# A hybrid decoder layer with the left pools of SBUF moved by 128 bytes, other homes for the split weights of the output projection, and an FFN issued stream by stream

## The chip, the cores and the metric

One core of a Trainium2 chip. The metric is the device time of one execution in microseconds; the time given for a kernel is the median of its runs.

## The reference

One layer over 1024 tokens of width 1024, in float32:

```python
h = rmsnorm(x, norm1_w) * (1 + scale1) + shift1          # scales, shifts, gates: silu(c) @ w_ada + b_ada
qa, ka, va, iq, ik, iw, qr, kr, vr, gr, ga, gb = split(h @ w_in)
y_a = sparse_attention(qa, ka, va, top 256 keys by iq, ik, iw) @ w_attn_proj
y_r = (silu(gr) * groupnorm(retention(qr, kr, vr))) @ w_ret_proj
x = x + gate1 * ((sigmoid(ga) * y_a + sigmoid(gb) * y_r) @ w_out)
h2 = rmsnorm(x, norm2_w) * (1 + scale2) + shift2
x = x + gate2 * ((silu(h2 @ w_ffn_gate) * (h2 @ w_ffn_up)) @ w_ffn_down)   # d_ff = 2816
return rmsnorm(x, final_norm_w)
```

## The kernel before

**Split operands.** Every large product is made of three matmuls on fp32r tiles: a float32 operand is split into a rounded part (`hi`, written by ACT) and the rest (`lo`, written by POOL or DVE), and hi·hi, hi·lo and lo·hi are summed in PSUM. Names that end in `hi` and `lo` are such parts. Nearly all of them are 128 x 128 stationary by 128 x 512 moving, called 512-column matmuls here.

**Who sets the order.** The kernel is written for a tile framework. A scheduler reorders the instructions of every engine, so the code's order is not the program's; each engine then runs its own list in order, and SP's list issues nearly all DMAs.

**Where tiles lie.** Pools grow from two ends of each partition's memory, "left" and "right". In the built program before, the tiles of the left pools that concern us (`whi`, `wlo`, `mhi`, `aT_hi`, `khi`, `fhi`, `flo`, `dw`, `wraw`) start at multiples of 256 bytes; the right pools' (`hT`, all slabs: `hc`, `early`, `late`, `raws`, `draw`, `dslot`) start 128 bytes after one. `qst`, in a left pool that is opened after some smaller tiles, also starts 128 bytes after one.

**Stages**, by the profile's time: condition vector and indexer projection to 123 us; indexer scores, projections from `w_in` (`hT` times `whi`, `wlo`) and retention with DVE's top-k to about 650; gates, retention projection and its normalisation (`gT`) to 907; attention to 1034; its projection to 1078; output projection (`w_out`) and second norm from 1083 to 1190; gate and up projections of the FFN from there to 1691; down projection to 1902.

**Output projection** (`for hf in range(2)`): `w_out` is loaded in 128 x 512 pieces to `wraw`, multiplied on POOL by the gate and split. The pieces of `hf` 0 use the ring of `whi`/`wlo` slots (`RING = 9`), which the attention's projection used before; of `hf` 1, four go to a slab tile `late`. `split_merged` makes `mhi` (ACT) and `mlo` (DVE), the other operand. In `hf` 1 each of the eight token tiles is normalised, transposed on PE and written by ACT to `hraw`.

**FFN, gate and up.** A Strassen-like scheme: `d_ff` is cut into 11 pairs, each with two streams (gate and up) of seven products (`ORDER` M1, M5, M6, M3, M7, M2, M4) of 12 matmuls. A product needs a combination of activations (`COMBOS`, tiles `hc`: h11, h21, S1, S2, h22, S4, S3) and a factor, 128 x 512 of weights or of differences of weights (`tmp`, by DVE, from `raws`), split to `fhi` (ACT) and `flo` (POOL), of which there are four slots each. M1 and M2 of pairs 0 and 1 are computed ahead: pair 0's factors (`early`) lie in slab 0 and are split while the output projection runs; pair 1's are split at the FFN's start into `fhi`/`flo` slots. The combinations S1 to S4 need the last token tile; DVE computes the sums (`hs`), ACT and POOL or DVE split them.

**What ends a pair.** `gu_finish` applies silu (ACT), multiplies gate by up (DVE), forms the four sums of activations for the down projection's own scheme and stores seven tiles to DRAM (`act_d`). `down_weights` loads a pair of rows of `w_ffn_down` to the one `dw` buffer (two loads of 512 KB), combines them in four DVE subtractions (L1167 to L1170) and stores 1 MB (`dw_d`). In the program the scheduler has put all eleven of these between about 1325 and 1460 us.

**Down projection.** `draw` loads, splits to `dslot` (ACT L1240; POOL or DVE L1241), products M1, M5, M6, M3, M7, M4, then M2, then the final norm (`sqh` squares, `rs3`).

Of the kernel before, what the change touches and what calls it, by code (L numbers as in the profile page):

```python
# [16 lines left out]
P = 128  # L17
# [24 lines left out]
def tile_hybrid_layer(ctx: ExitStack, tc: tile.TileContext, x, c, w_ada, b_ada, norm1_w, w_in,  # L42
# [20 lines left out]
    def f32(ap):  # L63
        return ap.bitcast(F32)
# [3 lines left out]
    def split_weight(raw, n, order=None):  # L68
        hi = ring.tile([P, H], R, name="whi", tag="whi", bufs=RING)
        lo = ring.tile([P, H], R, name="wlo", tag="wlo", bufs=RING)  # L70
# [8 lines left out]

    def raw_tile():  # L80
        return ring.tile([P, H], F32, name="wraw", tag="wraw", bufs=3)
# [779 lines left out]
    RING = 9  # L861
# [45 lines left out]
    COMBOS = {"h11": 3, "h21": 4, "S1": 1, "S2": 6, "h22": 0, "S4": 5, "S3": 2}  # L907
# [16 lines left out]
    hraw = [slab_tile(i, [P, 2, 4, H], F32, f"hraw{i}") for i in (2, 5)]  # L924
# [50 lines left out]
    def slab_slots():  # L975
        t = slab_tile(0, [P, 4, 2, H], R, "early")
        return lambda i: (four(t[:, i, 0, :]), four(t[:, i, 1, :]))

    for hf in range(2):
        cs = slice(hf * H, (hf + 1) * H)  # L980
        slots = []
        late = slab_tile(6, [P, 4, 2, H], R, "late") if hf else None
        for k in range(KT):
            if hf and k < 4:
                raw = raw_tile()
                nc.sync.dma_start(out=raw, in_=w_out[k * P:(k + 1) * P, cs])
                nc.gpsimd.tensor_mul(raw, raw, gate[:, cs])
                nc.scalar.activation(late[:, k, 0], raw, AF.Copy)
                nc.gpsimd.tensor_sub(late[:, k, 1], raw, f32(late[:, k, 0]))
                slots.append((late[:, k, 0], late[:, k, 1]))  # L990
            else:
                slots.append(rows_slot([(w_out, hf * H, H)], k, H, gate[:, cs]))
# [4 lines left out]
        for t in range(NT):  # L997
# [17 lines left out]
            for g in range(2):  # L1015
                xn = ring.tile([P, H], F32, name="xn2", tag="wraw", bufs=3)
# [11 lines left out]
            if t == 4:  # L1028
                early_load(0)
                early_split(0, slab_slots())  # L1030
            if t == 5:
                early_load(1)
    st_f.close()
# [95 lines left out]


# [58 lines left out]
    for p in range(2):  # L1189
        if p:  # L1190
            early_split(p, lambda i: factor_slot())
# [197 lines left out]
```

## Time and profile before

| | us |
|---|---|
| median of 3 runs | 1902.97 (1902.75 to 1904.68) |
| profiled execution | 1911.45 |
| its span | 1909.7 |
| PE busy in the span | 1781.0 (93%) |
| POOL, DVE, ACT busy | 898.0, 1183.3, 699.6 |

The profiled execution is one run with the hardware profiler on. Its span runs from the first to the last recorded instruction, and 1.75 us of its time lie outside. PE's mean granted clock is 0.975 of full speed. "Idle before" in square brackets is the time an engine did nothing ahead of a row, with what ended it.

### The profile page before, as it was taken

What the parts mean: (1) busy time and instruction counts of PE and PEld (TensorE: products, weight loads), DVE (VectorE), ACT (ScalarE), POOL (GpSimd) and SP (SyncE); (2) the same over time, 40 slices, a digit from 0 to 9 for tenths busy, and PEclk for the clock granted to TensorE, in tenths of its full rate; (3) what the DMA queues carried; (4) which work ended last, traced back from release to release, by engine and by line L of the source; (5) the groups of instructions that cost most, each with busy time, mean ns of one, the idle gap of its engine ahead of it and who ended that gap; (6) DMA issues with size and microseconds to landing.
All of it is one profiled execution on the core that took longest, in us unless ns stands there. A gap on an engine that the chain in (4) does not pass through costs nothing. (4 is left out here: it accounts for less than half of the span.)

```text
span 1909.7 us, 24906 instructions
## 1 busy us (share of the span) xinstructions
PE 1781.0 (93%) x8534; PEld 1445.4 (76%) x8534; DVE 1183.3 (62%) x1989; ACT 699.6 (37%) x1413; POOL 898.0 (47%) x954
## 2 busy tenths in 40 slices
PE   5899999999999998979899999599889999999997
PEld 4798888888888776867678787477667777788886
DVE  7646459999989784142665645856555444375554
ACT  3435432333322121210674246433233333354434
POOL 4572114665844372210463614844334444475585
PEclk9999999999999998989999999799999999999999
DMA  9443222122122775684944500235665333187652
GB/s 290 145 106 102 67 85 59 45 69 59 39 57 83 185 228 164 183 224 139 240 103 154 199 1 23 66 111 204 226 220 176 95 104 94 66 282 220 183 176 99
DMA packets 192286, 256.53 MB, mean 134 GB/s; under 512 B 29528, under 2 KB 126240, under 8 KB 189728
## 3 DMA queue, kind: packets, MB, share of 16 engines
q1 hardware_dynamic: 192160, 254.94, 43.8%
q8 instruction: 67, 1.10, 0.2%
q14 instruction: 59, 0.48, 0.1%
HBM read 190.67 MB, written 64.23 MB: 133 GB/s over the span
## 5 line engine op out<-in xcount | busy, mean ns | idle before, releaser
L73 POOL TENSOR_TENSOR wlo<-wraw,whi 128x512 fp32r<-128x512 f32 (+3 forms) x164 | 200.4, 1231 | 342.8 <-ACT whi L72 322.7
L108 PE MATMUL mm<-whi,hT_hi 128*128 128x512 f32 (+2 forms) x624 | 235.4, 379 | 7.1 <-ACT whi L72 6.0
L109 PE MATMUL mm<-wlo,hT_hi 128*128 128x512 f32 (+2 forms) x624 | 231.0, 370 | 0.8 <-POOL wlo L73 0.8
L110 PE MATMUL mm<-whi,hT_lo 128*128 128x512 f32 (+2 forms) x624 | 231.3, 371 | 0.0
L953 POOL TENSOR_TENSOR flo<-tmp,fhi 128x512 fp32r<-128x512 f32 x88 | 118.8, 1351 | 158.2 <-ACT fhi L952 126.2
L419 DVE MAX8 m<-score 128x8 f32<-128x384 f32 (+5 forms) x192 | 170.6, 891 | 4.7
L1111 PE MATMUL ya<-hc,fhi 128*128 128x512 f32 x344 | 140.1, 407 | 31.0 <-ACT fhi L952 20.6
L422 DVE MATCH_REPLACE8 score<-m,score 128x384 f32<-128x384 f32 (+5 forms) x192 | 168.1, 876 | 0.0
L72 ACT ACTIVATE whi<-wraw 128x512 fp32r<-128x512 f32 (+3 forms) x164 | 95.7, 593 | 192.4 <-DMA wraw<-in_w_in_dram 75.6
L1241 POOL TENSOR_TENSOR dslot<-draw,dslot 128x512 fp32r<-128x512 f32 x77 | 112.8, 1473 | 64.0 <-ACT dslot L1240 63.8
L108 PEld LDWEIGHTS mm<-whi,hT_hi 128*128 128x128 f32 x624 | 118.7, 190 | 27.2 <-ACT whi L72 6.6
L1113 PE MATMUL ya<-hc,fhi 128*128 128x512 f32 x344 | 139.0, 404 | 0.0
L1115 PE MATMUL ya<-hc,flo 128*128 128x512 f32 x344 | 136.3, 401 | 0.3 <-POOL flo L953 0.3
L115 PE MATMUL mm<-hT_hi,whi 128*128 128x512 f32 x328 | 123.8, 409 | 13.0 <-DVE qk_split L620 7.3
L953 POOL TENSOR_TENSOR flo<-raws,fhi 128x512 fp32r<-128x512 f32 x62 | 87.2, 1409 | 102.0 <-ACT fhi L952 102.0
L109 PEld LDWEIGHTS mm<-wlo,hT_hi 128*128 128x128 f32 x624 | 118.8, 190 | 20.6 <-POOL wlo L73 1.6
L110 PEld LDWEIGHTS mm<-whi,hT_lo 128*128 128x128 f32 x624 | 118.6, 190 | 19.6
L1241 DVE TENSOR_TENSOR dslot<-draw,dslot 128x512 fp32r<-128x512 f32 x77 | 79.5, 1047 | 84.4 <-ACT dslot L1240 74.4
L1240 ACT ACTIVATE dslot<-draw 128x512 fp32r<-128x512 f32 x154 | 89.4, 625 | 107.3 <-PE ya L1257 42.7
L117 PE MATMUL mm<-hT_lo,whi 128*128 128x512 f32 x328 | 124.8, 404 | 1.2 <-POOL hT_lo L247 1.2
L119 PE MATMUL mm<-hT_hi,wlo 128*128 128x512 f32 x328 | 123.5, 402 | 0.0
L952 ACT ACTIVATE fhi<-tmp 128x512 fp32r<-128x512 f32 x88 | 55.6, 631 | 177.9 <-PE yb L1113 69.6
(321 smaller groups left out, 4339.8 us busy)
## 6 DMA issues: line engine op xcount, KB each, us to landing
draw<-act_d SPq DMA_DIRECT2D x77, 256.0 KB
mw<-in_w_ada_dram SPq DMA_DIRECT2D x32, 512.0 KB
act_d<-c SPq DMA_DIRECT2D x62, 256.0 KB
wraw<-in_w_in_dram SPq DMA_DIRECT2D x56, 256.0 KB
wraw<-in_w_in_dram SPq DMA_DIRECT2D x96, 128.0 KB
raws<-in_w_ffn_gate_dram SPq DMA_DIRECT2D x24, 512.0 KB
raws<-in_w_ffn_up_dram SPq DMA_DIRECT2D x24, 512.0 KB
dw<-in_w_ffn_down_dram SPq DMA_DIRECT2D x22, 512.0 KB
```

Source lines behind the costliest of these rows:

```text
L73: nc.gpsimd.tensor_sub(lo[:, :n], raw[:, :n], f32(hi[:, :n]))
L108: nc.tensor.matmul(ps, lhsT=ahi, rhs=whi[:, :n], start=(i == 0), stop=False)
L109: nc.tensor.matmul(ps, lhsT=ahi, rhs=wlo[:, :n], start=False, stop=False)
L110: nc.tensor.matmul(ps, lhsT=alo, rhs=whi[:, :n], start=False, stop=(i == last))
L117: nc.tensor.matmul(ps, lhsT=whi, rhs=alo, start=False, stop=False)
L419: ins = nc.vector.max(m8, sc)
L422: nc.vector.match_replace(out=sc, in_to_replace=m8, in_values=sc, imm_value=TAKEN)
L953: nc.gpsimd.tensor_sub(lo, src, f32(hi))
L1111: nc.tensor.matmul(ps, lhsT=whi[:, k, :], rhs=hhi[:, k, :], start=first, stop=False, skip_group_check=True)
L1113: nc.tensor.matmul(ps, lhsT=whi[:, k, :], rhs=hlo[:, k, :], start=False, stop=False, skip_group_check=True)
L1115: nc.tensor.matmul(ps, lhsT=wlo[:, k, :], rhs=hhi[:, k, :], start=False, stop=last, skip_group_check=True)
L1241: lo_eng.tensor_sub(slot[:, 1], raw, f32(slot[:, 0]))
```

## The change

**Addresses.** `rs3`, a 64-byte tile in the first left pool, has four buffers for two. All left pools behind it start 128 bytes later: in the built program, the tiles of the left pools listed above start 128 bytes after a multiple of 256, as the right ones do (which have not moved). `qst` now starts at a multiple of 256, `khi` 128 after one.

**Output projection.** The pieces of `hf` 0 are split into slabs 2 and 5 (`wslot`), those of `hf` 1 into the ring, now of 8; `wraw` has four buffers for three. `hraw` takes slabs 2 and 5 only after that. Pair 1's early factors are split into slab 6 at token tile 5, and the slabs of S2, h22, S4 and S3 change places.

**FFN.** S4 has tiles of its own. Each stream's loads are issued one stream ahead. What ended a pair is spread: `after` applies silu or the multiplication behind the product that completes a block, and `finish_tasks` and `down_weights` queue the rest in `todo`, of which two are issued behind each later product.

**End.** `sqh` takes its buffers from the twelve `quad` tiles; second halves and norms of M4's tiles are issued after all four sums.

```diff
-    def split_weight(raw, n, order=None):
-        hi = ring.tile([P, H], R, name="whi", tag="whi", bufs=RING)
-        lo = ring.tile([P, H], R, name="wlo", tag="wlo", bufs=RING)
+    def split_weight(raw, n, order=None, home=None):
+        if home is not None:
+            hi, lo = home[:, 0], home[:, 1]
+        else:
...
-    RING = 9
+    RING = 8
+    N_RAW = 4
...
-    COMBOS = {"h11": 3, "h21": 4, "S1": 1, "S2": 6, "h22": 0, "S4": 5, "S3": 2}
+    COMBOS = {"h11": 3, "h21": 4, "S1": 1, "S2": 0, "h22": 6, "S4": 2, "S3": 5}
...
-    def slab_slots():
-        t = slab_tile(0, [P, 4, 2, H], R, "early")
+    def slab_slots(p):
+        t = slab_tile((0, 6)[p], [P, 4, 2, H], R, "early")
...
-        late = slab_tile(6, [P, 4, 2, H], R, "late") if hf else None
+        homes = [slab_tile(i, [P, 4, 2, H], R, "wslot") for i in (2, 5)] if hf == 0 else None
         for k in range(KT):
...
+            raw = raw_tile()
+            nc.sync.dma_start(out=raw, in_=w_out[k * P:(k + 1) * P, cs])
+            nc.gpsimd.tensor_mul(raw, raw, gate[:, cs])
+            home = homes and homes[k // 4][:, k % 4]
+            slots.append(split_weight(raw, H, home=home))
...
             if t == 5:
                 early_load(1)
+                early_split(1, slab_slots(1))
...
+        def after(self, m):
+            done = {"M3": "12", "M7": "22", "M2": "11", "M4": "21"}.get(m)
+            for c in [done] if done else []:
+                if c == "11" and self.p < 2:
+                    continue
+                self.use(c)
+            if m == "M4":
+                if self.p < 2:
+                    self.use("11")
+                if self.u:
+                    finish_tasks(self.p)
+        def use(self, c):
+            if self.u == 0:
+                src = self.A if c == "21" else self.c[c]
+                if c == "21":
+                    self.c[c] = quad_tile("c21")
+                nc.scalar.activation(self.c[c], src, AF.Silu)
+            else:
+                a = streams[self.p, 0].c[c]
+                nc.vector.tensor_mul(a, a, self.A if c == "21" else self.c[c])
...
-    def gu_finish(p, g, u):
-        a = {}
-        for b in ("12", "22", "11"):
-            nc.scalar.activation(g.c[b], g.c[b], AF.Silu)
-            nc.vector.tensor_mul(g.c[b], g.c[b], u.c[b])
-            a[b] = g.c[b]
-        g21 = quad_tile("g21")
-        nc.scalar.activation(g21, g.A, AF.Silu)
-        nc.vector.tensor_mul(g21, g21, u.A)
-        for m, b in (("M1", "11"), ("M2", "12"), ("M4", "22")):
-            act_store(p, m, a[b])
+    todo = []
+    def finish_tasks(p):
+        g, u = streams[p, 0], streams[p, 1]
+        a = g.c
         s1, s2, s3, s4 = u.c["11"], u.c["12"], u.c["22"], quad_tile("s4")
-        nc.vector.tensor_add(s1, g21, a["22"])
-        act_store(p, "M5", s1)
-        nc.vector.tensor_sub(s2, s1, a["11"])
-        act_store(p, "M6", s2)
-        nc.vector.tensor_sub(s3, a["11"], g21)
-        act_store(p, "M7", s3)
-        nc.vector.tensor_sub(s4, a["12"], s2)
-        act_store(p, "M3", s4)
+        todo.append(lambda: nc.vector.tensor_add(s1, a["21"], a["22"]))
+        todo.append(lambda: nc.vector.tensor_sub(s2, s1, a["11"]))
+        todo.append(lambda: nc.vector.tensor_sub(s3, a["11"], a["21"]))
+        todo.append(lambda: nc.vector.tensor_sub(s4, a["12"], s2))
+        for m, t in (("M1", a["11"]), ("M2", a["12"]), ("M4", a["22"]), ("M5", s1), ("M6", s2), ("M7", s3),
+                     ("M3", s4)):
+            todo.append(lambda m=m, t=t: act_store(p, m, t))
+        for q in {0: (), 1: (0, 1)}.get(p, (p,)):
+            down_weights(q)
     def down_weights(p):
         dw = ffn.tile([P, 4, H], F32, name="dw", tag="dw")
-        for f in range(2):
-            nc.sync.dma_start(out=dw[:, 2 * f:2 * f + 2, :].rearrange("p a n -> p (a n)"),
-                              in_=w_ffn_down[(2 * p + f) * P:(2 * p + f + 1) * P, :])
         b11, b12, b21, b22 = (dw[:, i, :] for i in range(4))
-        nc.vector.tensor_sub(b11, b12, b11)
-        nc.vector.tensor_sub(b12, b22, b12)
-        nc.vector.tensor_sub(b22, b22, b11)
-        nc.vector.tensor_sub(b21, b21, b22)
-        nc.sync.dma_start(out=dw_d[p], in_=dw)
+        def load():
+            for f in range(2):
+                nc.sync.dma_start(out=dw[:, 2 * f:2 * f + 2, :].rearrange("p a n -> p (a n)"),
+                                  in_=w_ffn_down[(2 * p + f) * P:(2 * p + f + 1) * P, :])
+        if p > 1:
+            todo.insert(0, load)
+        else:
+            todo.append(load)
+        todo.append(lambda: nc.vector.tensor_sub(b11, b12, b11))
+        todo.append(lambda: nc.vector.tensor_sub(b12, b22, b12))
+        todo.append(lambda: nc.vector.tensor_sub(b22, b22, b11))
+        todo.append(lambda: nc.vector.tensor_sub(b21, b21, b22))
+        todo.append(lambda: nc.sync.dma_start(out=dw_d[p], in_=dw))
...
+    s3 = sums(h11, h12, ALU.subtract)
+    s4 = sums(h21, s2, ALU.subtract)
+    split_combo("S4", s4, nc.gpsimd)
     split_combo("h22", h22, nc.gpsimd)
-    for k in range(4):
-        nc.vector.tensor_sub(h21[k], h21[k], s2[k])
-    s3 = sums(h11, h12, ALU.subtract)
-    split_combo("S4", h21, nc.gpsimd)
     split_combo("S3", s3, nc.gpsimd)
...
+    for n in range(2, len(flow)):
+        st = flow[n]
...
+            flow[n + 1].open()
+        for m in ORDER:
+            if st.p > 1 or m not in EARLY:
+                st.product(m)
+                st.after(m)
+                for task in todo[:2]:
+                    task()
+                del todo[:2]
...
-        sq = ffn.tile([P, H], BF16, name="sqh", tag="tmp", bufs=4)
+        sq = ffn.tile([P, H], BF16, name="sqh", tag="quad", bufs=12)
...
-        rs = const.tile([P, 16], F32, name="rs3", bufs=2)[:, 0:1]
+        rs = const.tile([P, 16], F32, name="rs3", bufs=4)[:, 0:1]
```

What the scheduler made of it, at three places. First **PE where a pair ends**, well into the FFN: before, the last product (M4) of a stream in `ya_13570`, the end of M1's `yb_13753`, and M2 of the other stream in `yb_13828`. `fhi_13824` and `flo_13825` take the slots that `fhi_13681` and `flo_13682` leave.

```order
L1111 MATMUL ya_13570<-hc_11475,fhi_13681 128x512
L1113 MATMUL ya_13570<-hc_11475,fhi_13681 128x512
L1115 MATMUL ya_13570<-hc_11475,flo_13682 128x512
L1115 MATMUL yb_13753<-hc_11449,flo_13750 128x512
L1111 MATMUL yb_13828<-hc_10789,fhi_13824 128x512
L1113 MATMUL yb_13828<-hc_10789,fhi_13824 128x512
L1115 MATMUL yb_13828<-hc_10789,flo_13825 128x512
```

The same place with the change: M7 in `ya_13709`, M2 in `yb_13817`, M3's sum in `yb_13732`. `fhi_13813` takes the slot of a factor that was last used 14 matmuls earlier (2 matmuls earlier for M2 of the pair's other stream), `flo_13814` of one 26 earlier.

```order
L1120 MATMUL ya_13709<-hc_11452,flo_13752 128x512
L1116 MATMUL yb_13817<-hc_10782,fhi_13813 128x512
L1118 MATMUL yb_13817<-hc_10782,fhi_13813 128x512
L1116 MATMUL yb_13732<-hc_11477,fhi_13771 128x512
L1118 MATMUL yb_13732<-hc_11477,fhi_13771 128x512
L1120 MATMUL yb_13732<-hc_11477,flo_13772 128x512
...
L1120 MATMUL yb_13732<-hc_11477,flo_13772 128x512
L1120 MATMUL yb_13817<-hc_10782,flo_13814 128x512
L1116 MATMUL yb_13817<-hc_10782,fhi_13813 128x512
L1118 MATMUL yb_13817<-hc_10782,fhi_13813 128x512
```

Two matmuls of M2 that need `fhi` alone stand ahead of another product's twelve, and the first that needs `flo` behind them.

Second, **DVE at the start of the FFN**, before: `hraw_10361` and `hraw_10360` hold the normalised activations, L1177 and L1202 write sums, L1185 the lo part of S1, L1084 (two rows at the end) the first differences of weights for pair 0.

```order
L1098 TENSOR_TENSOR held<-held,yb 128x512
L1177 TENSOR_TENSOR hs<-hs,hraw_10360 128x512
L1177 TENSOR_TENSOR hs<-hraw_10360,hraw_10361 128x512 x4
L1202 TENSOR_TENSOR hraw_10360<-hraw_10360,hs 128x512 x3
L1185 TENSOR_TENSOR hc<-hs,hc 128x512
L1202 TENSOR_TENSOR hraw_10360<-hraw_10360,hs 128x512
L1185 TENSOR_TENSOR hc<-hs,hc 128x512 x3
L1084 TENSOR_TENSOR tmp<-raws 128x512
L1084 TENSOR_TENSOR tmp<-raws,tmp 128x512
```

With the change (L1208 for L1177, L1089 for L1084, `hraw_10739` and `hraw_10738` for the two):

```order
L1089 TENSOR_TENSOR tmp<-raws,tmp 128x512
L1208 TENSOR_TENSOR hs<-hraw_10739 128x512 x2
L1089 TENSOR_TENSOR tmp<-raws,tmp 128x512
L1208 TENSOR_TENSOR hs<-hraw_10739 128x512 x2
L1103 TENSOR_TENSOR held<-held,yb 128x512
L1208 TENSOR_TENSOR hs<-hs,hraw_10738 128x512
L1103 TENSOR_TENSOR held<-held,yb 128x512
L1208 TENSOR_TENSOR hs<-hs,hraw_10738 128x512 x2
L1089 TENSOR_TENSOR tmp<-raws 128x512
L1208 TENSOR_TENSOR hs<-hs,hraw_10738 128x512
L1208 TENSOR_TENSOR hs<-hraw_10738,hraw_10739 128x512 x4
```

The differences of weights stand ahead of and between the sums; the third and fourth sets of sums, and S1's lo part, stand behind them.

Third, **ACT at the start of the output projection**, before (L72 splits `hf` 0's pieces into the ring, L988 into `late`, L932 makes `mhi`):

```order
L824 ACTIVATE aT_hi<-pva 128x512
L72 ACTIVATE whi<-wraw 128x512 x6
L988 ACTIVATE late<-wraw 128x512
L72 ACTIVATE whi<-wraw 128x512
L988 ACTIVATE late<-wraw 128x512 x3
L932 ACTIVATE mhi<-merged_10015 128x512 x4
L72 ACTIVATE whi<-wraw 128x512
```

With the change (L75 for L72, L938 for L932, L958 splits pair 1's early factors):

```order
L829 ACTIVATE aT_hi<-pva 128x512
L75 ACTIVATE wslot<-wraw 128x512 x8
L958 ACTIVATE early<-raws 128x512 x4
L75 ACTIVATE whi<-wraw 128x512 x8
L938 ACTIVATE mhi<-merged_10015 128x512 x7
L1009 ACTIVATE ya,ssum<-x_10343 128x512
```

The eight pieces of `hf` 0 and the four early factors now stand ahead of the eight pieces that take ring slots, and all twenty ahead of `mhi`.

## Rows read from the trace of the kernel before

**Rows 1.** The page's first line, the span.
```profile
span 1909.7 us, 24906 instructions
```

**Rows 2.** Windows: busy us of each engine, granted clock, DMA share, GB/s.
```profile
core 0: us, PE busy (x) PEld busy (x) DVE busy (x) ACT busy (x) POOL busy (x), PEclk, DMA share, GB/s
130.00:650.00 520.00, 515.89 (x2343) 423.88 (x2342) 424.30 (x775) 186.06 (x411) 253.33 (x357) 1.00 0.28 75
1190.00:1235.00 45.00, 22.30 (x75) 15.60 (x72) 39.89 (x33) 21.86 (x42) 34.24 (x21) 0.73 0.19 58
1340.00:1690.00 350.00, 325.44 (x1328) 256.27 (x1328) 175.21 (x204) 117.96 (x204) 156.94 (x116) 0.96 0.44 146
1690.00:1740.00 50.00, 50.00 (x222) 41.35 (x221) 37.05 (x38) 25.24 (x43) 33.78 (x23) 1.00 0.85 279
```

**Rows 3.** Groups by shape on PE from 130 to 650 us.
```profile
L108 PE MATMUL mm<-whi,hT_hi 128*128 128x512 f32 x384 | 155.6, 407 | 0.0
...
L115 PE MATMUL mm<-hT_hi,whi 128*128 128x512 f32 x227 | 85.3, 400 | 3.2 <-DVE qk_split L620 3.2
...
L392 PE MATMUL lg<-khi,qst 128*128 128x512 f32 x40 | 15.8, 396 | 0.0
```

**Rows 4.** Timeline of PE, FFN products: first and last of 18 matmuls.
```profile
1599.95 0.40 PE L1111 MATMUL ya<-hc,fhi 128*128 128x512 f32 x1
...
1603.92 0.39 PE L1111 MATMUL ya<-hc,fhi 128*128 128x512 f32 x1
```

**Rows 5.** Timeline of PE, down projection: first and last of 20 matmuls.
```profile
1749.69 0.39 PE L1258 MATMUL ya<-dslot 128*128 128x512 f32 x1
...
1754.00 0.39 PE L1256 MATMUL ya<-dslot 128*128 128x512 f32 x1
```

**Rows 6.** Timeline of PE, early products: first and last of 9 matmuls.
```profile
1187.69 0.39 PE L1111 MATMUL yb<-hc,early 128*128 128x512 f32 x1
...
1189.50 0.39 PE L1115 MATMUL yb<-hc,early 128*128 128x512 f32 x1
```

**Rows 7.** Waits of PE, 1034 to 1909 us: total, times, longest.
```profile
PE ya L1111 <- ACT fhi L952: 20.6, 2, 16.6
PE yb L1115 <- POOL flo L953: 15.5, 9, 1.9
PE ya L1111 <- DVE c L1098: 9.3, 3, 4.9
```

**Rows 8.** Timeline where one pair ends, 1563 to 1567 us.
```profile
1564.82 1.71 POOL L953 TENSOR_TENSOR flo<-raws,fhi 128x512 fp32r<-128x512 f32 x1
...
1566.59 0.50 PE L1115 MATMUL yb<-hc,flo 128*128 128x512 f32 x1 [1.93 <-POOL flo L953]
```

**Rows 9.** Timeline of DVE at the start of the FFN.
```profile
1192.25 2.50 DVE L1177 TENSOR_TENSOR hs<-hraw 128x512 f32<-128x512 f32 x4 [6.04 <-ACT hraw L1023]
...
1200.38 6.90 DVE L1177 TENSOR_TENSOR hs<-hraw,hraw 128x512 f32<-128x512 f32 x4
...
1220.59 1.74 DVE L1084 TENSOR_TENSOR tmp<-raws 128x512 f32<-128x512 f32 x1
```

**Rows 10.** Timeline of PE at the start of the FFN.
```profile
1194.81 0.50 PE L1111 MATMUL ya<-hc,fhi 128*128 128x512 f32 x1 [4.04 <-ACT fhi L952]
...
1224.78 0.80 PE L1111 MATMUL ya<-hc,fhi 128*128 128x512 f32 x1 [16.56 <-ACT fhi L952]
```

**Rows 11.** Chain that ended last: first and last of eight loads of dw.
```profile
1340.84 7.29 DMA dw<-in_w_ffn_down_dram
...
1446.63 6.33 DMA dw<-in_w_ffn_down_dram
```

**Rows 12.** Timeline of ACT at the start of the output projection.
```profile
1081.87 0.63 ACT L988 ACTIVATE late<-wraw 128x512 fp32r<-128x512 f32 x1 [5.20 <-POOL wraw L987]
1082.40 2.17 ACT L932 ACTIVATE mhi<-merged 128x512 fp32r<-128x512 f32 x4
```

**Rows 13.** Timeline of DVE ahead of the last product of the down projection.
```profile
1866.67 3.48 DVE L1241 TENSOR_TENSOR dslot<-draw,dslot 128x512 fp32r<-128x512 f32 x2 [2.37 <-PE ya L1258]
```

More of the change, by code (lines that the diff above doesn't have):

```diff
@@ L66, in tile_hybrid_layer @@
     RING = 12
-    def split_weight(raw, n, order=None):
-        hi = ring.tile([P, H], R, name="whi", tag="whi", bufs=RING)
-        lo = ring.tile([P, H], R, name="wlo", tag="wlo", bufs=RING)
+    def split_weight(raw, n, order=None, home=None):
+        if home is not None:
+            hi, lo = home[:, 0], home[:, 1]
+        else:
+            hi = ring.tile([P, H], R, name="whi", tag="whi", bufs=RING)
+            lo = ring.tile([P, H], R, name="wlo", tag="wlo", bufs=RING)
         if order is None:
@@ L78, in split_weight @@
         return hi, lo
+    N_RAW = 3
     def raw_tile():
-        return ring.tile([P, H], F32, name="wraw", tag="wraw", bufs=3)
+        return ring.tile([P, H], F32, name="wraw", tag="wraw", bufs=N_RAW)
     def rows_slot(pieces, kt, n=H, scale=None):
@@ L923, in tile_hybrid_layer @@
     ssum = const.tile([P, NT, 2], F32, name="ssum")
-    hraw = [slab_tile(i, [P, 2, 4, H], F32, f"hraw{i}") for i in (2, 5)]
+    hraw = []
     def split_merged(t, gs=(0, 1)):
@@ L981, in tile_hybrid_layer @@
         slots = []
-        late = slab_tile(6, [P, 4, 2, H], R, "late") if hf else None
+        homes = [slab_tile(i, [P, 4, 2, H], R, "wslot") for i in (2, 5)] if hf == 0 else None
         for k in range(KT):
[L984 to L992, printed above, removed]
+            raw = raw_tile()
[3 more added lines that the diff above has]
+            slots.append(split_weight(raw, H, home=home))
+        if hf:
+            hraw = [slab_tile(i, [P, 2, 4, H], F32, f"hraw{i}") for i in (2, 5)]
         head = {}
@@ L1015, in tile_hybrid_layer @@
             for g in range(2):
-                xn = ring.tile([P, H], F32, name="xn2", tag="wraw", bufs=3)
+                xn = ring.tile([P, H], F32, name="xn2", tag="wraw", bufs=N_RAW)
                 nc.vector.tensor_scalar(xn, x1[t][:, g * H:(g + 1) * H], rs, None, op0=ALU.mult)
@@ L1029, in tile_hybrid_layer @@
                 early_load(0)
-                early_split(0, slab_slots())
+                early_split(0, slab_slots(0))
             if t == 5:
                 early_load(1)
+                early_split(1, slab_slots(1))
     st_f.close()
@@ L1189, in tile_hybrid_layer @@
     for p in range(2):
-        if p:
-            early_split(p, lambda i: factor_slot())
         for m in EARLY:
@@ L1199, in tile_hybrid_layer @@
     split_combo("S2", s2, nc.gpsimd)
+    s3 = sums(h11, h12, ALU.subtract)
+    s4 = sums(h21, s2, ALU.subtract)
+    split_combo("S4", s4, nc.gpsimd)
     split_combo("h22", h22, nc.gpsimd)
-    for k in range(4):
-        nc.vector.tensor_sub(h21[k], h21[k], s2[k])
-    s3 = sums(h11, h12, ALU.subtract)
-    split_combo("S4", h21, nc.gpsimd)
     split_combo("S3", s3, nc.gpsimd)
-    for p in range(NP):
-        g, u = (streams[p, i] for i in range(2))
-        rest = [m for m in ORDER if p > 1 or m not in EARLY]
-        if p == 0:
-            g.open()
-            u.open()
-            for m in rest:
-                g.product(m)
-                u.product(m)
-        else:
-            for s in (g, u):
-                s.open()
-                for m in rest:
-                    s.product(m)
-        gu_finish(p, g, u)
-        for q in {0: (), 1: (0, 1)}.get(p, (p,)):
-            down_weights(q)
+    flow = [streams[p, u] for p in range(NP) for u in range(2)]
+    flow[0].open()
+    flow[1].open()
+    for m in ORDER:
+        if m not in EARLY:
+            for st in flow[:2]:
+                st.product(m)
+                st.after(m)
+    for n in range(2, len(flow)):
+        st = flow[n]
+        if n == 2:
+            st.open()
+        if n + 1 < len(flow):
+            flow[n + 1].open()
+        for m in ORDER:
+            if st.p > 1 or m not in EARLY:
+                st.product(m)
+                st.after(m)
+                for task in todo[:2]:
+                    task()
+                del todo[:2]
+    for task in todo:
+        task()
     raw_ring = slab_tile(COMBOS["h11"], [P, 8, H], F32, "draw")
@@ L1309, in tile_hybrid_layer @@
                 add_out(pss[i], 4 + i, 0)
-                second_half(4 + i)
-                square(4 + i, 1, 0, H)
-                final_norm(4 + i, 1)
+    for i in range(4):
+        second_half(4 + i)
+        square(4 + i, 1, 0, H)
+        final_norm(4 + i, 1)
     factors = [down_factors("M2", p) for p in range(NP)]
```

## The prediction

> **What bounds the kernel now.** I took the span first [rows 1]: 1909.7 us, with 1.75 us outside it, so the profiled execution took 1911.45 us, 0.45% above the median of 1902.97. Sums below are of the profiled execution; I take the difference off the median, since the two differ by less than the uncertainty of the sum. The table has PE busy for 93% of the span, so there are two ways to gain: matmuls that follow each other faster, and stretches in which PE waits. The windows tell which stretch is which [rows 2]: from 130 to 650 us PE is busy for 515.89 of 520 us at full clock, with DVE at 424 of 520 behind it; at the start of the FFN (1190 to 1235) for 22 of 45, at a granted clock of 0.73; in the later pairs (1340 to 1690) for 325 of 350 at 0.96. The list of waits names who is late there [rows 7].
>
> **Spacing of matmuls.** A busy time of 400 ns says little, since matmuls overlap; their starts say more. In the FFN 18 matmuls start between 1599.95 and 1603.92 us, 17 steps of 233.5 ns [rows 4]. In the down projection 20 start in 4.31 us, 19 steps of 226.8 ns [rows 5]. Same form, same clock, no wait in either. In the first, one operand (`hc`) starts 128 bytes after a multiple of 256 and the other (`fhi`, `flo`) at one; in the second both are `dslot`, with the same remainder. Is it the remainder, or the two ends of memory? The early products take the same `hc` against `early`, also at 128, and run at 1.81 us for 8 steps, 226 ns [rows 6]; that fits both. `khi` and `qst` lie in pools of one end, at different remainders: their busy mean is 396 ns, as for `hT` against weights (400 and 407) [rows 3], which speaks for the remainder. I price a changed matmul at 6 ns, between 5 and 6.9 (233.5 less 226.6).
>
> [...]
>
> Counted:
> - FFN: 11 pairs x 2 streams x 7 products x 12 = 1848 matmuls, less the 48 of pair 0's early ones and 48 of pair 1's, which will use `early` as well but only now gain: 1800 x 6 ns = **10.8 us**. PE is what ends the FFN's work, so I take all of it.
> - 130 to 650 us: three lines of 384 matmuls and three of 228 ([rows 3] has one of each kind, with one record missing), 1836 x 6 ns = 11.0 us. DVE, at 82% over the stretch, is nearly as full in its middle, and part may turn into waiting for it: **8 us**, bounds 3 and 12.
> - Gates and retention projection (650 to 907) hold some 900 more, but PE waits there for loads and DVE: **1 us**. `khi`/`qst` stay apart (128 and 0). `late` goes: `wslot` against `mhi` now agree, 96 x 6 ns = **0.5 us**.
>
> **Where a pair ends.** PE waits 9 times for `flo`, 15.5 us in all, at most 1.9 each [rows 7]. In one of them POOL's `flo<-raws` starts at 1564.82, runs 1.71 us, and PE goes on at 1566.59, after 1.93 us idle [rows 8]. The order shows why: M2's factor takes the slots of M4's, used 2 matmuls earlier, so ACT and then POOL have to work while PE stands. With the change the `flo` slot was free 26 matmuls before, and M2's first two matmuls, which need `fhi` alone, are followed by another product's twelve (2.7 us) before `flo` is wanted. What remains is ACT's `fhi`, 0.3 to 0.5 us a pair, as now. Gain 8 pairs x 1.9 = **15 us**. The granted clock is below full behind some of the waits: 0.96 over the 350 us from 1340 to 1690 [rows 2] is 14 us of lost speed, which these pair ends and the waits for `dw` below share. With shorter waits I take **5 us** of it here, bounds 0 and 8.
>
> **Start of the FFN.** PE idles 4.04 us ahead of 1194.81, while pair 1's early factors are split, and 16.56 us ahead of 1224.78 [rows 10]; that is the 20.6 us of the first line of waits [rows 7]. The second wait is for `fhi` of pair 0's next factor, whose difference (`tmp`) DVE starts at 1220.59, behind 24 sums that began at 1192.25, four of which took 6.90 us while POOL was at work, 1.7 each, where the first four took 2.50 alone [rows 9]. With the change pair 1's 48 matmuls (11 us) need no further factor and can run at once. DVE then needs 12 operations from the first sum to the fourth of S2, differences of weights among them: between 12 x 0.62 = 7.5 us and 12 x 1.7 = 20 us; I take 13, POOL being busy for part of it. S2's lo part on POOL and M6's last matmuls end some 3 us later, at 16 us after 1192.25, M6 of the other stream 3 us after that. M5 needs S1's lo part, which stands behind four sums S3: ten operations of 1.3 us, so DVE is through 26 us after 1192.25 and M5 of both streams 30 us. At 32.5 us, where PE goes on today, 48 matmuls more are behind it: 11 us. S4 and S3 still have to be split on POOL, a wait of some us that today's order has in a similar place. Gain **11 us**, bounds 5 (20 us of sums) and 20 (both waits gone).
>
> **Weights of the down projection.** Their eight loads on the chain begin at 1340.84 and the last at 1446.63 [rows 11]: 15.1 us a cycle of load, four subtractions, store and next load in one buffer. Eleven cycles are needed; DVE's list now holds 3, 4, 3 and 1 of them in four pairs, and 3, 3, 3 and 2 in the change. PE's waits for DVE's `c` (9.3 us, [rows 7]) belong to this, and half of the 14 us of clock: 16 us. A pair takes 168 x 0.2266 = 38 us. In the change the four subtractions stand together or nearly so, without the one or two operations of 0.6 to 1.7 us that stand between them now, so I take 13.5 us for a cycle; three are 40.5 us, DVE is some 2.5 us late per pair, and 8 us in all remain. Gain **8 us**, bounds 0 (the cycle stays at 15.1) and 16. The scheduler still puts all loads early in SP's list.
>
> **Output projection and end.** ACT reaches `mhi` at 1082.40, behind the last `late` piece [rows 12]. In the change ten more POOL and ACT operations stand ahead of it, but eight of them (`wslot`) no longer wait for ring slots, so they begin right after the attention. POOL needs about 28 operations of 1.3 to 1.7 us (1.71 in [rows 8]) from the attention's end at 1034 on, 36 to 48 us, which ends at 1070 to 1082; then come `whi` and `mhi`. **1 us** gain, bounds -4 and 3. At the end, two subtractions of 1.74 us stand on DVE ahead of the addition that frees PE's bank [rows 13]; the order there has not changed, nor has the tail behind the last matmul: nothing.
>
> **Sum:** 10.8 + 8 + 1 + 0.5 + 15 + 5 + 11 + 8 + 1 = 60 us. 1903 - 60 = **1843 us**.
>
> **The rivals.**
> - *The starts of operands are not the cause.* 20 us of the sum fall away: 1863. For it: no single pair of tiles is measured at both remainders. Against it: five kinds of operands fall on the right side of the line [rows 3 to 6]. Chance 0.08.
> - *The FFN's start and the dw chain stay bound by DVE and POOL.* The same number of sums, splits and subtractions is done; only their order changes. Without these two terms 1843 + 19 = 1862. For it: DVE busy for 39.9 of 45 us and POOL for 34.2 [rows 2]. Against: PE waits there for a difference that needs none of the sums. Chance 0.2. That the scheduler undoes the steps is a part of it: DVE's list is much as before.
> - *Loads into the left pools get slower at 128 bytes.* By the rows, `draw` already lands at that remainder and moves 279 GB/s at a share of 0.85 [rows 2], no worse per share than the 75 at 0.28 of the loads to the left: price 0 to 6 us, so 1843 to 1849. [...] Chance 0.08.
> - *Slower: the cycle of dw grows.* Multiplications and stores of a pair now stand among the next pair's products, and SP's list in order; if a load of `dw` waits behind a store that waits for DVE, and DVE's subtraction for the load, each cycle loses more. All else gains 52 us, so it decides at 11 cycles x 4.8 us more than now, a cycle of about 20 us. At 22, the time is 1903 - 52 + 11 x 6.9 = 1927. Today's mean is 15.1 with four cycles in one of the pairs, so little speaks for it. Chance 0.06, with 0.04 more that another queue held up ends at no change.
>
> **How the numbers follow.** The sum as it stands has 0.54, within 1843 +- 15. The rivals above take 0.46. Adding the bounds of all terms would give 1821 to 1897; all bounds at once are unlikely, and the two rivals of 1862 belong in: **1823 to 1880**. What a measurement here can tell from no change is about 0.2%, 3.8 us. Faster 0.90, same 0.04, slower 0.06.
>
> **What would show it.** Matmuls of the FFN and of `hT` at 226 to 227 ns from start to start (233 would refute that step); no wait for `flo` over 0.5 us where a pair ends, clock near 1.00 over the later pairs; one PE wait of under 10 us between norm 2 and the third pair; waits for `c` of under 10 us while `dw` cycles; PE's wait ahead of M2 of the down projection unchanged. The prediction fails if the gain from the spacing shows up as longer waits of PE between 600 and 910 us, or if DVE's list, with subtractions among it, becomes what the FFN waits for.

## The result and the profile after

| us | before | after |
|---|---|---|
| median | 1903.2 (4 runs) | 1854.6 (4 runs, 1853.62 to 1856.76) |
| profiled execution | 1911.45 | 1856.76 |
| its span | 1909.7 | 1855.0 |
| PE busy in the span | 1781.0 (93%) | 1751.1 (94%) |

The ratio is 0.9745, with a 95% interval of 0.9728 to 0.9762: 48.6 us are gained where 60 were forecast. Between the two profiled executions it is 54.7 us of span; the one of before lay 8.2 us above its median now, that of after 2.2.

The page's first line, against [rows 1]:

```profile
span 1855.0 us, 24891 instructions
```

The windows, against [rows 2], with the same columns; the later ones are cut otherwise, since the FFN ends earlier.

```profile
130.00:650.00 520.00, 515.56 (x2366) 428.46 (x2365) 422.96 (x778) 186.44 (x413) 254.96 (x358) 0.99 0.28 77
1190.00:1240.00 50.00, 35.85 (x126) 26.03 (x125) 35.45 (x35) 21.10 (x38) 40.00 (x27) 0.83 0.22 68
1340.00:1640.00 300.00, 293.37 (x1267) 237.14 (x1266) 182.66 (x197) 109.56 (x191) 156.08 (x110) 0.99 0.48 161
```

From 130 to 650 us PE is as busy as before, but that busy time holds records of 23 matmuls more: the faster spacing doesn't show in the busy time, 515.56 us for 515.89. The FFN's start has PE busy for 35.85 of 50 us (22.30 of 45 before), and the later pairs run at a granted clock of 0.99 where it was 0.96.

Now PE's waits from 1030 to 1910 us, against [rows 7]; total, times and longest in us.

```profile
PE yb L1116 <- DVE held L1103: 10.5, 2, 9.6
PE ya L1290 <- DVE tmp L1298: 4.2, 1, 4.2
PE ya L115 <- DVE mlo L939: 3.9, 1, 3.9
PE ya L1116 <- DVE c L1103: 3.7, 4, 2.2
PE yb L1116 <- ACT fhi L958: 3.1, 9, 0.5
PE ya L1116 <- ACT c L1100: 2.1, 9, 0.2
```

The 15.5 us for `flo` at nine pair ends are gone, and so are the 20.6 us for `fhi` at the FFN's start. In that place stands a new wait of 9.6 us, for `held`, an addition of DVE. The waits for `c` fell from 9.3 to 3.7 us.

PE's timeline at five places: the output projection's start, the FFN's start, 18 matmuls in a row, one pair end, and the second product M2 of the down projection.

```profile
1071.42 0.50 PE L113 MATMUL ya<-wslot,mhi 128*128 128x512 f32 x1 [0.85 <-ACT mhi L938]
...
1072.28 0.39 PE L114 MATMUL yb<-wslot,mhi 128*128 128x512 f32 x1
1076.58 0.70 PE L115 MATMUL ya<-wslot,mlo 128*128 128x512 f32 x1 [3.92 <-DVE mlo L939]
...
1202.42 0.40 PE L1120 MATMUL ya<-hc,flo 128*128 128x512 f32 x1
1212.46 0.80 PE L1116 MATMUL yb<-hc,fhi 128*128 128x512 f32 x1 [9.65 <-DVE held L1103]
...
1558.05 0.39 PE L1120 MATMUL yb<-hc,flo 128*128 128x512 f32 x1
...
1561.90 0.39 PE L1120 MATMUL yb<-hc,flo 128*128 128x512 f32 x1
...
1577.09 0.39 PE L1120 MATMUL yb<-hc,flo 128*128 128x512 f32 x1
1577.74 0.50 PE L1116 MATMUL yb<-hc,fhi 128*128 128x512 f32 x1 [0.27 <-ACT fhi L958]
1578.08 0.40 PE L1118 MATMUL yb<-hc,fhi 128*128 128x512 f32 x1
1578.72 0.50 PE L1116 MATMUL ya<-hc,fhi 128*128 128x512 f32 x1 [0.24 <-ACT c L1100]
...
1815.24 0.77 PE L1290 MATMUL ya<-dslot 128*128 128x512 f32 x1 [4.18 <-DVE tmp L1298]
```

The starts from 1558.05 to 1561.90 are 17 steps of 226.5 ns; before it was 233.5 [rows 4]. At the pair's end two short gaps stand, 0.27 us for `fhi` and 0.24 for ACT's copy `c`, where the 1.93 us for `flo` stood [rows 8].

DVE's timeline while PE waits, against [rows 9]:

```profile
1185.40 1.30 DVE L1208 TENSOR_TENSOR hs<-hraw 128x512 f32<-128x512 f32 x2 [10.96 <-ACT hraw L1027]
...
1195.23 1.76 DVE L1208 TENSOR_TENSOR hs<-hs,hraw 128x512 f32<-128x512 f32 x1
1196.92 6.88 DVE L1208 TENSOR_TENSOR hs<-hraw,hraw 128x512 f32<-128x512 f32 x4
...
1209.33 1.28 DVE L1216 TENSOR_TENSOR hc<-hs,hc 128x512 fp32r<-128x512 f32 x2
...
1211.73 0.67 DVE L1103 TENSOR_TENSOR held<-held,yb 128x512 f32<-128x512 f32 x1
```

POOL's timeline there:

```profile
1201.52 6.74 POOL L1216 TENSOR_TENSOR hc<-hraw,hc 128x512 fp32r<-128x512 f32 x4
1213.67 4.76 POOL L959 TENSOR_TENSOR flo<-raws,fhi 128x512 fp32r<-128x512 f32 x2 [5.41 <-ACT fhi L958]
```

M5 needs two things: S1's lo part (DVE L1216, through at 1210.6) and a PSUM bank `yb`, which DVE's addition to `held` at 1211.73 gives back. Both stand behind the four sums S3 of 6.88 us, which no product needs so soon. POOL has nothing to do from 1208.26 to 1213.67.

### The profile page after: what moved, and what is told of

Same layout as the page of the kernel before. It is cut to its first block, busy times and chain, and to the rows that moved or that the text cites. A ratio compares the mean times of both kernels' runs of the same rounds, so it can differ in the third digit from the quotient of the medians.

```text
span 1855.0 us, 24891 instructions
## 1 busy us (share of the span) xinstructions
PE 1751.1 (94%) x8534; PEld 1436.9 (77%) x8534; DVE 1190.9 (64%) x1989; ACT 697.8 (38%) x1413; POOL 907.7 (49%) x954
## 5 line engine op out<-in xcount | busy, mean ns | idle before, releaser
L959 POOL TENSOR_TENSOR flo<-tmp,fhi 128x512 fp32r<-128x512 f32 x88 | 123.6, 1407 | 140.9 <-ACT fhi L958 102.0
L75 ACT ACTIVATE whi<-wraw 128x512 fp32r<-128x512 f32 (+3 forms) x160 | 93.1, 592 | 174.1 <-DMA wraw<-in_w_in_dram 70.2
L1116 PE MATMUL ya<-hc,fhi 128*128 128x512 f32 x336 | 132.8, 396 | 6.4 <-DVE c L1103 3.7
L1118 PE MATMUL ya<-hc,fhi 128*128 128x512 f32 x336 | 131.9, 392 | 0.9 <-POOL hc L1216 0.7
L1120 PE MATMUL ya<-hc,flo 128*128 128x512 f32 x336 | 131.5, 392 | 0.4 <-POOL flo L959 0.4
L1116 PE MATMUL yb<-hc,fhi 128*128 128x512 f32 x248 | 99.0, 402 | 13.8 <-DVE held L1103 9.6
```

The source lines that it names most:

```text
L959: nc.gpsimd.tensor_sub(lo, src, f32(hi))
L1116: nc.tensor.matmul(ps, lhsT=whi[:, k, :], rhs=hhi[:, k, :], start=first, stop=False, skip_group_check=True)
L1118: nc.tensor.matmul(ps, lhsT=whi[:, k, :], rhs=hlo[:, k, :], start=False, stop=False, skip_group_check=True)
L1120: nc.tensor.matmul(ps, lhsT=wlo[:, k, :], rhs=hhi[:, k, :], start=False, stop=last, skip_group_check=True)
```

## The experiments

**Addresses alone.** Three kernels are the one before with only the buffers of `rs3` changed, 64 bytes each, so that all left pools behind move and every instruction stays in its place: by 128 bytes with four buffers (`align_only`), by 256 with six (`shift_256`) and by 64 with three (`shift_64`). The first of them:

```diff
-        rs = const.tile([P, 16], F32, name="rs3", bufs=2)[:, 0:1]
+        rs = const.tile([P, 16], F32, name="rs3", bufs=4)[:, 0:1]
```

> The kernel before with four buffers of rs3 and nothing else: every engine's list is the same, all left pools start 128 bytes later. Remainder theory (two operands with the same remainder by 256 follow each other in 226 to 227 ns, others in about 232): matmuls of hT and of the FFN fall to 227 ns, khi with qst stay at 232, the time falls by 14 to 20 us to about 1886. [...] A mixture (spacing falls, but PE waits more behind it): the spacing falls and the time by less than 10 us.

> The kernel before with six buffers of rs3: left pools start 256 bytes later, remainders as before. Remainder theory: no change, 1903 within 3 us, spacing 232 in FFN and hT. If the move itself or the free buffers of rs3 bring the gain, it is that of four buffers, about 1886.

> The kernel before with three buffers of rs3: left pools start 64 bytes later, so left operands lie at 64 and right ones at 128 by 256. If equality is needed: no change, 1903 and 232 ns. If the cost grows with the distance: spacing near 229 ns and about half the gain of four buffers, 1894. dw loads and x loads then start at 64 too; if DMA minds, the start of the kernel gets later by 1 us or more.

First and last of 18 FFN matmuls in a row, PE's timeline in `align_only`:

```profile
1581.69 0.39 PE L1111 MATMUL ya<-hc,fhi 128*128 128x512 f32 x1
...
1585.55 0.39 PE L1115 MATMUL ya<-hc,flo 128*128 128x512 f32 x1
```

The same in `shift_256`:

```profile
1592.02 0.40 PE L1115 MATMUL ya<-hc,flo 128*128 128x512 f32 x1
...
1595.97 0.39 PE L1113 MATMUL yb<-hc,fhi 128*128 128x512 f32 x1
```

The same in `shift_64`:

```profile
1603.83 0.39 PE L1111 MATMUL ya<-hc,fhi 128*128 128x512 f32 x1
...
1607.72 0.39 PE L1115 MATMUL yb<-hc,flo 128*128 128x512 f32 x1
```

The steps are 227.1, 232.4 and 228.8 ns. The times: `align_only` 1884.31 us, ratio 0.9902 [0.9869, 0.9935], which is 18.6 us; `shift_256` 1902.12, 0.9998 [0.9978, 1.0018]; `shift_64` 1899.84, 0.9993 [0.9972, 1.0014]. So it is the remainder by 256 and not the move: a move by 256 changes nothing. In `align_only` the matmuls of `khi` and `qst`, which stay apart, step by 235 ns on average where it was 232, while `hT` and `hc` went from 232 to 227 or 228. The 64-byte move has the FFN at 229, `hT` at 230 where it is the moving operand and at 233 where it is the stationary one, and no time that can be told from no change.

One rival is left: that a tile at a multiple of 256 is slow in itself, and no likeness of the two operands is needed. The trace of before decides it. In the attention's projection both operands (`aT`, and `whi` or `wlo`) lie in left pools, at multiples of 256. First and last of 24 matmuls in a row:

```profile
1062.11 0.39 PE L115 MATMUL ya<-aT_hi,whi 128*128 128x512 f32 x1
...
1067.32 0.39 PE L119 MATMUL yb<-aT_hi,wlo 128*128 128x512 f32 x1
```

That is 226.5 ns a step, and 227 in `align_only` and `shift_64` too, where both move together. So what counts here is that the two remainders agree: 226.5 to 228 ns where they do, 232 and more where they lie 128 bytes apart.

**The alignment taken back.** `align_undone` is the changed kernel with two buffers of `rs3`.

```diff
-        rs = const.tile([P, 16], F32, name="rs3", bufs=4)[:, 0:1]
+        rs = const.tile([P, 16], F32, name="rs3", bufs=2)[:, 0:1]
```

> The changed kernel with two buffers of rs3: lists unchanged, left pools back at multiples of 256. If the terms add up: +17 us, as four buffers took off the kernel before, 1872. If part of the gain in the kernel before was lost in waits that are now gone: +19 to 23, 1874 to 1878.

1868.04 us, 0.9841 [0.9819, 0.9864]: 0.96% or 18 us slower than the changed kernel's ratio of 0.9745, 16 against the 0.9756 of its second measurement (`after_again`, below), and 13 by the medians. Within some 6 us the term is worth the same with the rest of the change and without it.

**Alignment and the FFN's new issue.** `flow_align` is the kernel before with `rs3` at four buffers and with `after`, `use`, `todo` and the loads one stream ahead; `w_out`'s homes, the slabs, pair 1's early factors, S4 and the end are as before.

```diff
-            for s in (g, u):
-                s.open()
-                for m in rest:
-                    s.product(m)
-        gu_finish(p, g, u)
...
+            flow[n + 1].open()
...
+                st.product(m)
+                st.after(m)
+                for task in todo[:2]:
+                    task()
+                del todo[:2]
```

> The kernel before with four buffers of rs3 and the new issue of the FFN (after, use, todo, streams one ahead), but with the homes of w_out, of pair 1's early factors, the slabs and S4 as before. By the terms: pair ends and dw as in the changed kernel (no wait for flo of 1.9 us at pair ends), the waits at the FFN's start as before (20 us, for fhi): 1903 - 17 - 12 - 10 - 6 of clock = 1858 to 1872. If the FFN's start depends on the order of issue and not on the homes, its wait falls too and the time is within 4 us of the changed kernel's 1854.6.

1866.34 us, 0.9801 [0.9761, 0.9841]. Beyond `align_only` this is 1.0% or 19 us; what is left to the whole change is 0.56%, 11 us. The intervals leave each of these open by 8 to 10 us. PE's waits from 1030 to 1910 us:

```profile
PE ya L1111 <- ACT fhi L952: 20.8, 3, 16.2
...
PE yb L1111 <- ACT fhi L952: 3.3, 9, 0.5
PE yb L1111 <- DVE c L1098: 3.1, 1, 3.1
...
PE ya L1111 <- DVE c L1098: 2.8, 1, 2.8
```

The FFN's start still waits its 16 and 4 us; no `flo` is waited for at a pair's end. So the parts are apart: pair ends and `dw` come from the new issue, the FFN's start from the other edits.

**Pair 1's early factors in the old slots.** `early_slots` is the changed kernel with these factors split at the FFN's start, to `fhi`/`flo` slots.

```diff
-                early_split(1, slab_slots(1))
...
     for p in range(2):
+        if p:
+            early_split(p, lambda i: factor_slot())
```

> The changed kernel, but pair 1's early factors are split at the FFN's start into fhi and flo slots, as before; S4's tiles, the slabs and the homes of w_out stay as changed. If the gain at the FFN's start comes from the 48 matmuls that can run at once, PE waits again some 4 us for the first fhi and over 12 us for the next factor: 1854.6 + 8 to 11 = 1863 to 1866. If it comes from S4's own tiles and the order of the sums: within 3 us of 1854.6.

1860.94 us, 0.9799 [0.9779, 0.9819]: 8 to 10 us more than the changed kernel by its two ratios. PE's timeline at the FFN's start:

```profile
1182.32 0.80 PE L1115 MATMUL ya<-hc,fhi 128*128 128x512 f32 x1 [4.05 <-ACT fhi L958]
1206.48 0.80 PE L1115 MATMUL ya<-hc,fhi 128*128 128x512 f32 x1 [11.59 <-ACT fhi L958]
1215.47 0.80 PE L1115 MATMUL yb<-hc,fhi 128*128 128x512 f32 x1 [7.76 <-DVE held L1102]
```

The two old waits for `fhi` are back, with the bank's wait behind them. This one edit carries the gain at the FFN's start: from its first to its last matmul the FFN takes 477.1 us here and 467.6 in the changed kernel.

**All tasks at once.** `at_once` issues the whole rest of a pair behind its last product; `open_same` opens each stream's loads at its own start. First `at_once`, then `open_same`:

```diff
-                for task in todo[:2]:
+                for task in todo:
                     task()
-                del todo[:2]
+                del todo[:]
```
```diff
-        if n == 2:
-            st.open()
-        if n + 1 < len(flow):
-            flow[n + 1].open()
+        st.open()
```

> The changed kernel, but all queued tasks of a pair are issued behind the pair's last product and not two behind each later product. If the steps bring the gain of the dw chain: DVE's list holds a pair's sums and dw subtractions in one piece, PE's waits for c grow by 5 to 10 us: 1860 to 1866. If the scheduler spreads them in any case: within 3 us of 1854.6.

> The changed kernel, but each stream's weights are asked for at its own start and not one stream ahead. If that lead matters, differences of weights come late, PE waits for fhi or c at the start of streams: 5 us or more above the changed kernel. If the scheduler moves the loads ahead in SP's list in any case: within 3 us.

`at_once` took 1879.78 us, 0.9902 [0.9881, 0.9923], 28 to 30 us more than the changed kernel by its two ratios and well above what was expected; `open_same` 1863.05, 0.9804 [0.9775, 0.9833], 9 us more than the changed kernel on the same chip (0.9756, below). Both steps matter, and the scheduler doesn't undo them. PE's waits in `at_once`, 1030 to 1910 us:

```profile
PE yb L1116 <- DVE c L1103: 8.4, 2, 4.9
PE yb L1116 <- ACT fhi L958: 8.4, 17, 0.5
PE yb L1120 <- POOL flo L959: 5.9, 9, 0.9
...
PE ya L1116 <- DVE c L1103: 4.0, 2, 2.2
```

Waits for `fhi` nearly tripled (9.3 us for 3.6), `flo` is waited for again at nine places (5.9 us), and DVE's `c` takes 12.4 us for 3.7. All of the loss lies in the FFN, which takes 496.0 us for 467.6.

**The waits that are left.** `three_fixes` is the changed kernel with three edits at waits of the profile after: M2 of the down projection sums in free banks, not in the one that DVE still reads; the head tiles of `w_out` do their matmuls with `mhi` first; M2 of pair 1 takes a `ty` bank. `sums_late` further writes S4, S3 and h22 ahead of the products that need them. Their diffs:

```diff
+    def m2_bank(i, n):
+        return (ps_b() if i < 2 else ps_ty()) if n == 0 else ps_a()
...
-            ps = ps_a()[:, :c1 - c0]
+            ps = m2_bank(i, n)[:, :c1 - c0]
...
-            mm_tok(head[t], split_merged(t, (0,)), slots, ks=range(4))
+            mm_tok(head[t], split_merged(t, (0,)), slots, ks=range(4), lo_last=True)
...
-            ps = self.B if m in ("M5", "M3") else ps_b() if m == "M2" else self.A
+            ps = self.B if m in ("M5", "M3") else (ps_ty() if self.p == 1 else ps_b()) if m == "M2" else self.A
```
```diff
-    s3 = sums(h11, h12, ALU.subtract)
-    s4 = sums(h21, s2, ALU.subtract)
...
+            if m == "M3":
+                s4 = sums(h21, s2, ALU.subtract)
+                split_combo("S4", s4, nc.gpsimd)
+            if m == "M7":
+                s3 = sums(h11, h12, ALU.subtract)
+                split_combo("S3", s3, nc.gpsimd)
```

> The changed kernel with three edits to waits that its trace shows. The last product of the down projection takes the two yb and two ty banks, which are free, so PE need not wait for the sum that frees ya: 4.2 us less, and up to 2 us of clock. The first tiles of the output projection do all products with mhi ahead of those with mlo, so that 16 matmuls and not 4 cover DVE's mlo: 2.5 to 3.5 us less. M2 of pair 1 takes the ty banks, so that M5 need not wait for DVE's addition to held: 2 to 6 us less, if S1's lo part, which DVE finishes 1 us earlier, does not take its place, in which case 1. In all 8 to 13 us: 1842 to 1847. If the waits only move on: 1850 to 1855.

> The three edits once more, beside the changed kernel on one chip. By the traces so far the waits they aim at fall by 2.9 us (mlo), some 1.5 (start of the FFN) and 5.4 (end): 9 to 10 us below the changed kernel. If the first ratio, 0.9719 against 0.9745, is all there is: 5 us.

> The changed kernel once more, on the chip that runs the next three: ratio 0.9745 within its interval. Its trace shows which stretches differ between two executions of one program; from the traces so far the stretch from 650 to 910 us and the start of the FFN's dw stretch differ by up to 6 us.

> The three edits, and the sums S4, S3 and the split of h22 written ahead of the products that need them, which puts S1's lo part on DVE ahead of eight sums. PE's wait of 5.6 us for DVE's hc at the FFN's start goes, its wait of 4.6 us for ACT's copy may stay; S2's last lo part now stands on POOL behind four of h22, 6.8 us, which could give 3 us back. 2 to 8 us below the three edits. If DVE and POOL have simply too much work there, the waits move to M3 and M7, and nothing is gained.

`three_fixes` took 1846.22 us, 0.9719 [0.969, 0.9748]. Once more, on one chip with the changed kernel: 1845.57, 0.9703 [0.9679, 0.9728], against 1855.41, 0.9756 [0.9732, 0.978] for `after_again`. It is 10 us below the changed kernel and the fastest here. `sums_late` took 1846.48, 0.9703 [0.9678, 0.9727], no better. PE's timeline at the FFN's start, and the start of the output projection, in `three_fixes`:

```profile
1080.01 0.39 PE L115 MATMUL yb<-wslot,mhi 128*128 128x512 f32 x1
1081.39 1.20 PE L121 MATMUL ya<-wslot,mlo 128*128 128x512 f32 x4 [0.99 <-DVE mlo L945]
...
1205.97 0.79 PE L1124 MATMUL yb<-hc,fhi 128*128 128x512 f32 x1 [5.59 <-DVE hc L1222]
1220.89 0.79 PE L1122 MATMUL ya<-hc,fhi 128*128 128x512 f32 x1 [4.63 <-ACT c L1106]
```

The same in `sums_late`:

```profile
1191.37 0.61 PE L1124 MATMUL yb<-hc,fhi 128*128 128x512 f32 x1 [2.96 <-DVE hc L1222]
1213.43 1.22 PE L1122 MATMUL yb<-hc,fhi 128*128 128x512 f32 x2 [10.17 <-ACT hc L1221]
```

With the bank free, M5 waits for S1's lo part (5.59 us), and a wait of 4.63 comes behind it. With the sums later, that falls to 2.96, and the sums that were put off, with ACT's split of them, are late by 10.17 us. The FFN's start stays bound by DVE's and POOL's work (43.1 and 42.9 us busy of the 50 from 1190 to 1240 in `three_fixes`): its waits move on, and the FFN from its first to its last matmul took 467.6 us in the changed kernel and 466.1 in `three_fixes`. By these traces the 10 us come from the other two edits, which were not run apart: the output projection took 92.8 us for 97.4 (the wait for `mlo` fell from 3.9 to 1.0), the down projection 206.2 for 211.6 (the wait of 4.2 ahead of its M2 is gone). The traces of `three_fixes_again` and `after_again` agree: 92.9 for 98.5, 206.1 for 209.4, and the FFN 468.0 for 467.3.

## Why the forecast held, and where it was off

The measured 1854.6 us lie inside the range, but nearer to the rivals' 1862 than to the sum's 1843. So it is the runs and not the time that decide between them.

**Spacing of matmuls: right in cause and total, not in where it pays.** 20.3 us were counted in four stretches; `align_only` gives 18.6 and `align_undone` 13 to 18. The rival that the remainders are not the cause falls: with every instruction in its place the FFN's step was 232.4 ns in `shift_256` and 227.1 in `align_only`. That the gain comes back as longer waits between 600 and 910 us didn't happen: the stretch to 640 us ended 6 us earlier than in the trace of before, that from there to 907 took 3.7 less (8 and 1 forecast). In the FFN, though, the step "PE is what ends the FFN's work, so I take all of it" failed by half: 1800 matmuls at 5.6 ns less are 10 us, but the FFN's length fell by 4.8 us from `align_undone` to the changed kernel (472.4 to 467.6) and by 5.5 from `shift_256` to `align_only` (508.9 to 503.4). In the first pair most of the rest came back as longer waits for DVE's `c`, 1.3 us (2.4 to 3.7), and as matmuls at a lower granted clock, some 3 (0.83 for 0.86 from 1190 to 1240 us, 0.99 for 1.00 from 1340 to 1460). That the total still came near is in part luck: in the traces the gates' 3.7 us for 1 made up for some of it.

**Where a pair ends: right in kind, a little too large.** No `flo` is waited for at a pair's end. The forecast left one gap there, for `fhi`; two remain, 0.65 and 0.64 us from start to start in the pair shown, where matmuls follow in 0.227: 0.42 and 0.41 lost, and in other pairs up to 1.06 together. The second, for ACT's copy `c`, is new. Before it was about 2.5 in most pairs, the 1.93 us idle among it [rows 8], but less in two of the nine. Over the whole FFN what these gaps for `flo`, `fhi` and ACT's `c` cost beyond an ordinary step fell from 21.7 us to 10.2: 11.5 us; 15 were counted.

**The cycle of `dw` and the clock: right in kind, too large.** DVE's first subtraction for `dw` (L1198) begins at 1288.1 us and the eleventh at 1426.2, ten cycles of 13.8; 13.5 were taken. By the same starts it was 14.7 before, not the 15.1 that the last eight loads gave. Against the trace of before, the waits for `c` fell by 5.6 us (9.3 to 3.7), and at a clock of 0.99 over 300 us some 3 us are lost where it was 14, so 11 more: 16.6 where 8 and 5 were counted. Against `shift_256`, a second record of the kernel before (next paragraph), it is 2.3 us of waits (6.0 to 3.7) and some 7.5 of clock: 10 where 13 were counted. `flow_align` can't say more: the three terms of the new issue, 15, 5 and 8, make 28, and it measured 19 beyond the alignment, with an uncertainty of some 10 from the two intervals.

**What was mis-sized, and why.** One step that failed stands ahead of the sum: that the difference between the profiled execution and the median could be passed over. `shift_256` is a second record of the same instructions with the same spacing, and its median is that of before. Its waits for `c`, from PE's list for 1030 to 1910 us:

```profile
PE ya L1111 <- DVE c L1098: 6.0, 3, 3.2
```

And its window, against [rows 2]:

```profile
1340.00:1690.00 350.00, 328.75 (x1354) 259.29 (x1354) 181.65 (x210) 120.54 (x207) 162.21 (x119) 0.97 0.44 151
```

That is 6.0 us of waits against 9.3 [rows 7]; the clock is 0.97 against 0.96 [rows 2], by two digits another 3.5 us; and its FFN, from the first matmul with `hc` to the last, takes 508.9 us against 514.7. So some 6 us of waits and clock that the sum removed look like that one execution's own, in the terms for `dw` and the clock; two records are few to say so. From trace to trace the FFN gave 47.1 us, where its five terms (spacing, pair ends, clock, start, `dw`) were 49.8, and all the program 54.7 for 60. In the medians it is 48.6, 6 less. Against `shift_256` the FFN gave 41.3 for the 49.8: the pair ends fell short by 3.5, the start by 1 to 3, `dw` and the clock by 3, which is where the lost half of the spacing shows. The sentence on the bounds of all terms is summed wrongly too: those stated give 1817 to 1872, not 1821 to 1897.

**Start of the FFN: right, 11 against 8 to 10.** The 8 to 10 are `early_slots`. At 32.5 us after the first sum 135 matmuls of the FFN had started where it was 96 in the trace of before: 39 more, where 48 were counted. DVE was to be through S1's lo part 26 us after its first sum, and was after 25.2 (1185.40 to 1210.6). What ended PE's wait was not that part but a bank, some 1.8 us later; `three_fixes` shows the named part right beneath.

**Output projection and end: within the bounds, by another wait.** A gain of 1 us was forecast and none measurable came: PE waits 0.85 us for `mhi`, where it was 4.5, but four matmuls on it waits 3.92 for `mlo`, which DVE makes. I had followed ACT's list and not DVE's. The wait ahead of M2 at the end is 4.2 us, for 4.3 before, and 2.8 in `after_again` and `shift_256`: it changes with the execution, not with the kernel.

**The other rivals.** That the FFN's start and the `dw` chain stay bound by DVE and POOL, at 1862, is true of what is left: at the start each wait that was removed uncovered the next (`three_fixes`, `sums_late`). As a forecast of no gain it is refuted: the start gave 8 to 10 us, and the cycle of `dw` fell from 14.7 to 13.8. That the scheduler undoes the steps is refuted by `at_once` and `open_same`: the order in the code is worth 28 to 30 and 9 us. Slower loads were not seen: the loads to the left pools moved 77 GB/s at a share of 0.28, where it was 75 at 0.28 [rows 2]. The 6 us at the upper end of that rival's price, and with them its 1849, come from no row, and no run shows them. The cycle of `dw` became shorter, so the slower rival never began.

**What stays open.** Which waits make up the 28 to 30 us of `at_once` was not taken apart to the end: its listed waits grew by some 20 and its FFN by 28.4; the clock was not costed. Why half of the FFN's spacing came back as waits and clock was read from traces and not tested. `flow_align` shows the whole new issue at once; pair ends, clock and `dw` were not run one by one.

## What to carry over

Look at the starts of matmuls, not at their busy time: where two stretches of one form at full clock stepped differently here (233.5 and 226.8 ns), the operands' addresses were behind it, and a tile of 64 bytes aligned everything behind it. Work that ends a unit was best issued in small steps among the next unit's products (28 to 30 us here), and loads one unit ahead (9 us), even where a scheduler reorders. A sum made on one profiled execution inherits its bad luck; where it lies above the median, take a second record before cutting its waits.

## What the runs showed of the hardware

- Matmuls of 128 x 128 by 128 x 512 at full clock started every 226 to 228 ns when both operands began at the same remainder by 256 bytes (both 0 for `aT` with `whi` in the trace of before, both 128 for the FFN in `align_only`), and every 232 to 236 when they lay 128 apart (`hc` with `fhi` in the trace of before, `khi` with `qst` in those of both kernels). At 64 apart (`shift_64`) the FFN's took 229, those of `hT` 230 as the moving operand and 233 as the stationary one; no run here tells why these differ.
- In the changed kernel two of DVE's sums `hs` of 128 x 512 took 1.30 us at 1185.40 with POOL idle, 0.65 each, and four took 6.88 at 1196.92 beside POOL's work, 1.72 each.
